# Gates of two streams packed into one half-width tile, and low parts at the GLU's start moved to GpSimd

## The chip, the cores and the metric

One core of a Trainium2 chip runs the whole kernel. The metric is the device time of one execution in microseconds (us), the median of several; less is better. The engines go by the profile's names: PE is TensorE's matmul and PEld its weight load, DVE is VectorE, ACT is ScalarE, POOL is GpSimd, SP is SyncE, whose queue (SPq) issues the DMAs.

## The reference

Two layers run over two streams, a latent of 256 tokens and a context of 256 tokens, both 1024 wide. Layer 0 mixes with a bidirectional S5 state-space scan followed by a GLU, layer 1 with a bidirectional gated DeltaNet over chunks of 64 tokens with 16 value heads. Each layer ends with a squared-ReLU MLP (the context's only in layer 0). The pieces that the change touches:

```python
# S5 layer, for each stream
y = gelu(y_forward + y_backward + d_skip * u)
y_a, y_b = split(y @ w_glu, 2);  out = y_a * sigmoid(y_b)
# gated DeltaNet layer, for each stream: 4 x 16 gate columns of w_in
gl = rest[..., qk + vd:].reshape(b, l, 2, 2, 16)      # (beta | g) x (forward | backward) x head
beta = sigmoid(gl[:, :, 0])
g = -exp(a_log) * softplus(gl[:, :, 1] + dt_bias)
g_b = cumsum(blocks(g), axis=-1)                      # within chunks of 64 tokens
```

## The kernel before

Matmuls run in a 32-bit format of reduced precision, so every operand is split in a high part and a low part (the rest), and every product is three matmuls (`mm3`: high by high, high by low, low by high). The high part is a cast on ScalarE, the low part a subtraction on VectorE or GpSimd.

**Order.** The kernel is written as tasks (generators). `drive` advances the task whose next step could start first by a clock of estimated durations (`Clock`), with priorities; each engine gets its instructions in the order that this and the tile framework's scheduler give, and works through them in that order. So an instruction that waits holds up all that is queued behind it on its engine. In the DeltaNet stage the clock also fills gaps in an engine's estimated time.

**Start of the GLU (some 205 to 330 us).** `y_split(s, b)` splits block b (of 8) of stream s of the S5 output, yT, into yh (ScalarE) and yl (VectorE) for all 16 (s, b); s = 0 is the context. `w_load` loads the 32 GLU weight blocks on SP's queue into four buffers (wraw), `w_split` makes whi on ScalarE and wlo in two halves of 128 x 512, the first on GpSimd, the second on VectorE (`loeng`). `glu(0, ...)` then takes weight blocks in order; one block meets two of the eight yT blocks, 12 matmuls of 512 columns. At the same time `s5_out(b, 1)` brings out the latent's eight blocks: TensorE, VectorE (sum, transposes, copies of states Hs) and ScalarE (GELU).

**Start of the DeltaNet stage (some 738 us on).** `w_load`, `w_split` and `gdn_proj` run through 48 projection blocks of 128 columns, the gates' own block third, after the first two query blocks. A projection of both streams takes 512 columns a matmul, of the latent alone 256; the gates' block does its two streams one after the other, in the order (1, 0), each with 24 matmuls of 256 columns into its half of one PSUM bank. The block has 4 groups of 32 rows, of which the upper 16 are zero columns of the weights: beta forward, beta backward, g forward, g backward, 16 heads each. Convolution and SiLU of each projection (`conv_silu`: four multiply-adds cacc and four or two products on VectorE, the rest on ScalarE) free the PSUM bank.

`gdn_gates` works on 128 x 512 tiles (tiles named gt; columns are the context's 256 tokens, then the latent's 256): log-sigmoid and softplus by exp, a reciprocal and a polynomial on VectorE; scans along the tokens, one for each direction; four DMAs write the summed decays GR to DRAM (grd); four transposes (gtp) and 32 small matmuls (glp, decays at the chunks' ends) go through PSUM, and VectorE copies them out. From the gates' block on, GpSimd makes all low parts of the weights in four quarters (`alone`). Behind the gates, `gdn_t(p, d)` computes for each head pair p and direction d a triangular inverse: it reads X from grd by DMA, GpSimd adds a mask, VectorE subtracts (X, gpn), and with the keys' products (kks, from transposes of the keys that share PSUM banks with gtp and glp) N, U and T follow in turns between VectorE, TensorE and ScalarE. `gdn_chain` runs the recurrences over the chunks, `gdn_read` and `gdn_out` the readout; the second MLP ends the kernel.

Of the kernel before, what the change touches and what calls it, by code (L numbers as in the profile page):

```python
# [978 lines left out]
def host_weights(i):  # L979
    a = {n: np.asarray(v) for n, v in i.items()}  # L980
    out = {}
    w = a["s5_w_glu"][0].reshape(8, 128, 2, 4, 256)
    out["w_glu"] = w.transpose(3, 0, 1, 2, 4).reshape(4, 4, 2, 128, 512).transpose(0, 1, 3, 2, 4).reshape(4, 4, 128, 1024)
    out["w1"] = a["mlp_w1"].reshape(2, 4, 2, 128, 8, 512).transpose(0, 4, 1, 3, 2, 5).reshape(2, 8, 4, 128, 1024)
    out["w2"] = a["mlp_w2"].reshape(2, 8, 4, 128, 1024)
    wi = a["gdn_w_in"][0]
    out["w_in"] = wi[:, :6144].reshape(8, 128, 48, 128).transpose(2, 1, 0, 3).reshape(48, 128, 1024)
    wg = np.zeros((1024, 4, 32), np.float32)
    wg[:, :, :16] = wi[:, 6144:].reshape(1024, 4, 16)
    out["w_gate"] = wg.reshape(8, 128, 128).transpose(1, 0, 2).reshape(128, 1024)  # L990
    gb = np.zeros((2, 4, 32), np.float32)
    gb[0, 2:, :16] = a["gdn_dt_bias"][0]
    gb[1, 2:, :16] = a["gdn_a_log"][0]
# [25 lines left out]
class K2(K):  # L1019
# [100 lines left out]
    def w_split(self, blocks):  # L1120

        nc = self.nc
        for _, shape, *dst in blocks:
            if not dst:
                yield from self.hslot.take()
            while not self.raws:
                yield HOLD
            raw, _, t = self.raws.pop(0)
            yield t
            hi, lo = dst or [self.wr.tile([128, 1024], F32R, name=n, tag=n, bufs=self.nhi) for n in ("whi", "wlo")]  # L1130
            nc.scalar.copy(hi, raw)

            n = 4 if self.loeng[0] is self.loeng[1] is nc.gpsimd else 2
            for j in range(n):
                h = slice(j * 1024 // n, (j + 1) * 1024 // n)
                self.loeng[2 * j // n].tensor_tensor(lo[:, h], raw[:, h], hi[:, h].bitcast(F32), op=OP.subtract)
            self.wslot.give()
            (self.wout if dst else self.wq).append([t.rearrange("p (a b) -> p a b", a=shape[0]) for t in (hi, lo)])
            yield
# [8 lines left out]
    def y_split(self, s, b):  # L1148
# [6 lines left out]
        nc.vector.tensor_tensor(nat(self.yl), src, nat(self.yh).bitcast(F32), op=OP.subtract)  # L1155
# [126 lines left out]
def s5_phase(ctx, k):  # L1282

    nc = k.nc
    with ExitStack() as cs:
# [119 lines left out]
        ld, sp = T(k.w_load(blocks), 0, [], "sync"), T(k.w_split(blocks), 0, [], "scalar")  # L1405
# [22 lines left out]
def host_consts2():  # L1428
# [17 lines left out]
    c[:, M_G] = np.where(r % 32 >= 16, 0.0, np.where(r < 64, -1.0, 1.0))  # L1446
    c[:, M_G + 1] = (r % 32 < 16) & (r >= 64)
# [9 lines left out]
class K3(K2):  # L1457
# [48 lines left out]
    def gdn_gates(self, tmp, o):  # L1506
# [7 lines left out]
        def t():  # L1514
            tag = next(room)
            return (self.gb.tile([128, 512], F32, name="gt", tag=tag) if tag == "N" else
                    self.gw.tile([128, 512], F32, name="gt", tag=tag, bufs=NRB))
# [4 lines left out]
        V.tensor_scalar(s, ps, gs, gc[:, 0:1], op0=OP.mult, op1=OP.add)  # L1522
# [30 lines left out]
        for d in range(2):  # L1553
            r = slice(64 + 32 * d, 96 + 32 * d)
            G.memset(m[r], 1.0)
            G.memset(m[r, (0 if d == 0 else 63):512:64], 0.0)
            f = lambda x: x[r] if d == 0 else bass.AP(tensor=x.tensor, offset=x[r].offset + 511, ap=[list(x[r].ap[0]), [-1, 512]])
# [12 lines left out]
        for k in range(8):  # L1570
            for d in range(2):
                c = k if d == 0 else (3 - k if k < 4 else 11 - k)
                last = c * 64 + (63 if d == 0 else 0)
                o = k * 32 + d * 16
                nc.tensor.matmul(lp[:, o:o + 16], GR[64:128, last:last + 1].to_broadcast([64, 128]),
                                 self.ident[64:128, 64 + 32 * d:64 + 32 * d + 16], start=(k == 0 and d == 0), stop=(k == 7 and d == 1),
                                 skip_group_check=True)
        gt = t().rearrange("p (a b c d) -> p a b c d", a=4, b=2, c=2)
        V.tensor_copy(gt.rearrange("p a b c d -> p (a b c d)"), tp)
# [4 lines left out]
        V.tensor_tensor(self.gp, gt[:, :, 1, :, 0:16], gt[:, :, 0, :, 0:16], op=OP.subtract)  # L1584
# [4 lines left out]
        V.tensor_copy(gn, gt[:, :, 1, :, 0:16])  # L1589
# [19 lines left out]
    def gdn_proj(self, streams, out):  # L1609

        while not self.wq:
# [6 lines left out]
        for n, s in enumerate(streams):  # L1618
            o = ps if s is None else ps[:, 256 * s:256 * s + 256] if len(streams) > 1 else ps[:, 0:256]
            for dt in range(8):  # L1620
                self.mm3(o, wh[:, dt], wl[:, dt], self.cols(self.hh, dt, s), self.cols(self.hl, dt, s), dt == 0, dt == 7)
# [424 lines left out]
    def gdn_phase(self, tmp, gb, hp, new):  # L2046
# [42 lines left out]
        def gate():  # L2089
            j = proj(I["w_gate"], (1, 0), 0, o)  # L2090
# [174 lines left out]
```

## Time and profile before

| | us |
|---|---|
| median of 3 runs | 1602.71 |
| lowest, highest | 1600.59, 1606.34 |
| profiled execution | 1608.33 |
| its span | 1606.5 |
| PE busy (share of span) | 1461.4 (91%) |
| DVE busy | 1098.4 (68%) |
| ACT busy | 775.2 (48%) |
| POOL busy | 652.0 (41%) |

The rows below were taken from the profiled execution; times in them count from its span's start. In a timeline a row is a run of like instructions: start, time until the last ends, engine, line, operation, output and inputs with shapes, count, and in brackets the idle time before it and who ended it. All instructions carry line L273, that of the helper that issues them, so groups go by the names of tiles. A waits view says who waited for whom. PE's busy time contains overlaps of pipelined matmuls.

### The profile page before, as it was taken

The page shows a single profiled execution, that of the slowest core. Times are in us where ns is not written, and L with a number is a line of the kernel's source. Part 1 is how long each engine was busy: PE and PEld are TensorE (multiplying, and loading weights), DVE is VectorE, ACT ScalarE, POOL GpSimd, SP SyncE. Part 2 cuts the span into 40 slices and gives each one's busy share as a digit, 9 for nine tenths or more (in the row PEclk, how much of TensorE's full clock was granted, in tenths as well). Part 3 has the DMA queues.
Part 4 walks back from the last instruction along what each step waited for, and adds up shares of the span by engine and source line. Part 5 has one row for each costly group of instructions (what it writes and reads, how often), then busy time and mean ns, then how long its engine had stood idle before and what let it go on. Part 6 is the DMA issues. An engine that isn't in the chain of part 4 may idle for free. (4 is left out here: it accounts for less than half of the span.)

```text
span 1606.5 us, 31329 instructions
## 1 busy us (share of the span) xinstructions
PE 1461.4 (91%) x12370; PEld 1115.2 (69%) x12370; DVE 1098.4 (68%) x2036; ACT 775.2 (48%) x1635; POOL 652.0 (41%) x590
## 2 busy tenths in 40 slices
PE   6895689989999999996978998989998999989998
PEld 2474457768777777786756775767776665789997
DVE  6999877754334333448998876686978775666766
ACT  3262675534222223315456655656665755564443
POOL 4962026623333332335777543443543400024432
PEclk8897789989999999998889999989998999999999
DMA  8758725454444454422222211111121112535552
GB/s 286 255 195 200 141 86 184 151 183 134 163 162 166 163 187 161 152 91 66 90 70 67 67 54 48 50 51 54 61 70 38 45 58 79 188 127 194 185 186 92
DMA packets 76771, 200.77 MB, mean 125 GB/s; under 512 B 8784, under 2 KB 29008, under 8 KB 76368
## 3 DMA queue, kind: packets, MB, share of 16 engines
q1 hardware_dynamic: 76112, 197.78, 38.3%
q8 instruction: 97, 1.59, 0.4%
q10 hardware_dynamic: 512, 0.98, 0.2%
q14 instruction: 50, 0.41, 0.1%
HBM read 192.71 MB, written 6.03 MB: 124 GB/s over the span
## 5 line engine op out<-in xcount | busy, mean ns | idle before, releaser
L273 ACT CAST whi<-wraw 128x1024 fp32r<-128x1024 f32 x221 | 225.6, 1045 | 255.7 <-PE w L273 139.0
L273 POOL TENSOR_TENSOR wlo<-wraw,whi 128x256 fp32r<-128x256 f32 (+1 forms) x221 | 206.8, 963 | 270.7 <-ACT whi L273 253.2
L273 DVE TENSOR_TENSOR wlo<-wraw,whi 128x1024 fp32r<-128x1024 f32 (+1 forms) x189 | 223.4, 1210 | 81.5 <-ACT whi L273 80.6
L273 PE MATMUL w<-hh,whi 128*128 128x256 f32 (+1 forms) x512 | 170.4, 335 | 0.0
L273 PE MATMUL w<-hl,whi 128*128 128x256 f32 (+1 forms) x512 | 169.3, 332 | 0.0
L273 PE MATMUL w<-hh,wlo 128*128 128x256 f32 (+1 forms) x512 | 168.9, 332 | 0.0
L273 POOL TENSOR_TENSOR sq<-rl 128x512 f32<-128x512 f32 (+1 forms) x64 | 62.7, 980 | 216.1 <-ACT rl L273 212.1
L273 PE MATMUL w<-whi,h1h 128*128 128x512 f32 x384 | 148.9, 395 | 0.0
L273 PE MATMUL w<-whi,h1l 128*128 128x512 f32 x384 | 148.5, 390 | 0.0
L273 PE MATMUL w<-wlo,h1h 128*128 128x512 f32 x384 | 148.4, 389 | 0.0
L273 PE MATMUL proj<-hh,whi 128*128 128x256 f32 (+1 forms) x360 | 132.4, 368 | 7.4 <-ACT pp L273 6.7
L273 DVE TENSOR_TENSOR ma<-w,g 128x512 f32<-128x512 f32 x96 | 65.3, 687 | 103.0 <-PE w L273 102.9
L273 PE MATMUL proj<-hh,wlo 128*128 128x256 f32 (+1 forms) x360 | 127.8, 355 | 1.2 <-POOL wlo L273 1.2
L273 PE MATMUL proj<-hl,whi 128*128 128x256 f32 (+1 forms) x360 | 127.3, 354 | 0.0
L273 POOL TENSOR_TENSOR xr<-xr,ma 128x512 f32<-128x512 f32 x56 | 82.2, 1471 | 95.1 <-DVE ma L273 95.1
L273 DVE SCALAR_TENSOR_TENSOR cacc<-pp,cw,cacc 128x520 f32<-128x520 f32 (+1 forms) x128 | 112.3, 879 | 9.6 <-ACT cacc L273 8.0
L273 ACT ACTIVATE v<-c,vsc 64x128 f32<-64x128 f32 x224 | 80.7, 362 | 62.8 <-PE c L273 57.7
L273 PEld LDWEIGHTS w<-hh,whi 128*128 128x128 f32 x512 | 98.0, 192 | 18.3 <-DVE wlo L273 4.2
L273 DVE TENSOR_TENSOR h1l<-sq,h1h 128x512 fp32r<-128x512 f32 (+1 forms) x64 | 36.3, 568 | 104.5 <-POOL sq L273 102.1
L273 PEld LDWEIGHTS w<-hl,whi 128*128 128x128 f32 x512 | 98.5, 192 | 10.5 <-issue 1.9
L273 PEld LDWEIGHTS w<-hh,wlo 128*128 128x128 f32 x512 | 98.3, 192 | 9.8 <-issue 0.8
L273 POOL TENSOR_TENSOR rstd<-ms,mhalf 128x1 f32<-128x1 f32 (+2 forms) x22 | 17.3, 788 | 179.1 <-DVE ms L273 163.4
(316 smaller groups left out, 3492.2 us busy)
## 6 DMA issues: line engine op xcount, KB each, us to landing
wraw<-in_w_dram SPq DMA_DIRECT2D x128, 512.0 KB, 4.5
adaw<-in_ada_w_dram SPq DMA_DIRECT2D x92, 512.0 KB, 4.8
wraw<-in_w_in_dram SPq DMA_DIRECT2D x48, 512.0 KB, 3.2
wraw<-in_w_glu_dram SPq DMA_DIRECT2D x32, 512.0 KB, 3.4
wraw<-in_w_out_dram SPq DMA_DIRECT2D x16, 512.0 KB, 3.4
Kt<-kd SPq DMA_DIRECT2D x32, 128.0 KB, 6.5
X<-grd SPq DMA_DIRECT2D x32, 128.0 KB, 3.2
V<-in_ada_w_dram SPq DMA_DIRECT2D x4, 512.0 KB, 5.2
```

The costliest lines, as they stand in the source:

```text
L273: r = f(*args, **kw)
```

## The change

**Gates.** The weights' zero columns change places with the used ones: in each group of 32 the used 16 are now the upper 16. For the latent (s = 1) the matmul takes the block's 128 columns as they are; for the context (s = 0) it takes a window that begins 16 columns later, so the context's gates land in rows 0 to 15 of each group and the latent's in rows 16 to 31, each meeting zeros of the other. Both streams accumulate into one 128 x 256 region; the last window is 112 columns wide. The order of the streams is (0, 1). All tiles of `gdn_gates` are 256 columns wide; the scans cover 256 tokens of both streams at once; the DMAs into grd are eight (one for each direction, parity and stream) with half the data; the transposes are two; two operations on the transposed gates (gp, gn) are done for each stream.

**GLU.** `y_split` makes the context's low parts on GpSimd, the latent's on VectorE as before. `w_split(blocks, 3)` makes both halves of the first three GLU weight blocks' low parts on GpSimd.

```diff
-    wg[:, :, :16] = wi[:, 6144:].reshape(1024, 4, 16)
+    wg[:, :, 16:] = wi[:, 6144:].reshape(1024, 4, 16)
...
-                self.loeng[2 * j // n].tensor_tensor(lo[:, h], raw[:, h], hi[:, h].bitcast(F32), op=OP.subtract)
+                (nc.gpsimd if nb < first else self.loeng[2 * j // n]).tensor_tensor(lo[:, h], raw[:, h], hi[:, h].bitcast(F32), op=OP.subtract)
...
-        nc.vector.tensor_tensor(nat(self.yl), src, nat(self.yh).bitcast(F32), op=OP.subtract)
+        (nc.vector if s else nc.gpsimd).tensor_tensor(nat(self.yl), src, nat(self.yh).bitcast(F32), op=OP.subtract)
...
-        ld, sp = T(k.w_load(blocks), 0, [], "sync"), T(k.w_split(blocks), 0, [], "scalar")
+        ld, sp = T(k.w_load(blocks), 0, [], "sync"), T(k.w_split(blocks, 3), 0, [], "scalar")
...
-                    self.gw.tile([128, 512], F32, name="gt", tag=tag, bufs=NRB))
+                    self.gw.tile([128, 512], F32, name="gt", tag=tag, bufs=NRB))[:, 0:256]
...
-        V.tensor_scalar(s, ps, gs, gc[:, 0:1], op0=OP.mult, op1=OP.add)
+        V.tensor_scalar(s, ps[:, 0:256], gs, gc[:, 0:1], op0=OP.mult, op1=OP.add)
...
-            G.memset(m[r, (0 if d == 0 else 63):512:64], 0.0)
+            G.memset(m[r, (0 if d == 0 else 63):256:64], 0.0)
...
-                r = 64 + 32 * d + h2
-                dst = bass.AP(tensor=self.grd.tensor, offset=self.grd.offset + 8192 * d + 64 * h2, ap=[[1024, 8], [128, 8], [1, 64]])
-                nc.sync.dma_start(dst, GR[r:r + 16:2].rearrange("p (c i) -> p c i", i=64))
+                for s in range(2):
+                    r = 64 + 32 * d + 16 * s + h2
+                    dst = bass.AP(tensor=self.grd.tensor, offset=self.grd.offset + 8192 * d + 64 * h2 + 512 * s, ap=[[1024, 8], [128, 4], [1, 64]])
+                    nc.sync.dma_start(dst, GR[r:r + 15:2].rearrange("p (c i) -> p c i", i=64))
...
-        for b in range(4):
+        for b in range(2):
             nc.tensor.transpose(tp[:, b * 128:b * 128 + 128], GR[:, b * 128:b * 128 + 128], self.ident)
...
-        V.tensor_tensor(self.gp, gt[:, :, 1, :, 0:16], gt[:, :, 0, :, 0:16], op=OP.subtract)
+        for s in range(2):
+            V.tensor_tensor(self.gp[:, 2 * s:2 * s + 2], gt[:, :, 1, :, s], gt[:, :, 0, :, s], op=OP.subtract)
...
-        V.tensor_copy(gn, gt[:, :, 1, :, 0:16])
+        for s in range(2):
+            V.tensor_copy(gn[:, 2 * s:2 * s + 2], gt[:, :, 1, :, s])
...
-            o = ps if s is None else ps[:, 256 * s:256 * s + 256] if len(streams) > 1 else ps[:, 0:256]
+            o = ps if s is None else ps[:, 0:256]
...
+                    wide = 128 if s or dt < 7 else 112
+                    lh, ll = [w.rearrange("p a b -> p (a b)")[:, 128 * dt + 16 - 16 * s:128 * dt + 16 - 16 * s + wide] for w in (wh, wl)]
+                    for m, (l, x) in enumerate(((lh, self.hh), (lh, self.hl), (ll, self.hh))):
+                        nc.tensor.matmul(o[0:wide], l, self.cols(x, dt, s), start=n == dt == m == 0, stop=n == 1 and dt == 7 and m == 2,
+                                         skip_group_check=True)
...
-            j = proj(I["w_gate"], (1, 0), 0, o)
+            j = proj(I["w_gate"], (0, 1), 0, o)
```

## Rows read from the trace of the kernel before

**Rows 1.** the page's busy times: busy us, share of the span, instructions

```profile
PE 1461.4 (91%) x12370; PEld 1115.2 (69%) x12370; DVE 1098.4 (68%) x2036; ACT 775.2 (48%) x1635; POOL 652.0 (41%) x590
```

**Rows 2.** busy time by stretch: us, then PE, PEld, DVE, ACT, POOL busy

```profile
753.00:786.00 33.00, 29.39 (x154) 24.54 (x152) 31.22 (x40) 16.36 (x37) 29.02 (x37) 0.95 0.24 82
786.00:805.00 19.00, 18.83 (x90) 15.86 (x90) 18.72 (x35) 10.21 (x26) 9.08 (x9) 0.82 0.26 85
805.00:825.00 20.00, 12.89 (x75) 9.95 (x74) 17.77 (x21) 10.41 (x22) 17.81 (x16) 0.90 0.25 79
825.00:850.00 25.00, 20.91 (x223) 17.62 (x222) 23.14 (x39) 14.75 (x34) 15.79 (x18) 0.81 0.15 47
```

**Rows 3.** waits of PE from 805 to 850: us, times, longest

```profile
PE ap L273 <- DVE T L273: 6.3, 2, 3.6
PE proj L273 <- ACT pp L273: 3.5, 1, 3.5
```

**Rows 4.** waits of PE from 204 to 262

```profile
PE glu L273 <- ACT whi L273: 1.9, 2, 1.2
PE glu L273 <- POOL wlo L273: 1.5, 2, 1.1
PE yp L273 <- ACT Hs L273: 0.7, 1, 0.7
```

**Rows 5.** busy time of the gate tiles alone, 753 to 806

```profile
753.00:806.00 53.00, 5.52 (x36) 5.20 (x36) 24.33 (x27) 1.05 (x2) 1.26 (x4) 0.90 0.25 82
```

**Rows 6.** groups of VectorE's instructions, shapes apart, 753 to 806

```profile
L273 DVE SCALAR_TENSOR_TENSOR gt<-gt 128x512 f32<-128x512 f32 x9 | 9.4, 1044 | 0.2
L273 DVE RECIPROCAL gt<-gt 128x512 f32<-128x512 f32 x1 | 3.4, 3353 | 0.0
L273 DVE TENSOR_TENSOR_SCAN gt<-gt 32x512 f32<-32x512 f32 x2 | 3.2, 1610 | 0.1
L273 DVE SCALAR_TENSOR_TENSOR zs<-zth,proj 128x256 f32<-128x256 f32 x1 | 0.4, 406 | 0.0
```

**Rows 7.** timeline of VectorE: start, us, instruction

```profile
796.14 0.68 DVE L273 TENSOR_TENSOR X<-X,gpn 128x512 f32<-128x512 f32 x1
803.27 0.42 DVE L273 COPY gt<-glp 128x256 f32<-128x256 f32 x1
813.18 1.82 DVE L273 TENSOR_TENSOR N<-X,kks 128x512 f32<-128x512 f32 x2
```

**Rows 8.** timelines of VectorE, TensorE, SP's queue and GpSimd

```profile
743.29 1.37 DVE L273 TENSOR_TENSOR hl<-hf,hh 128x512 fp32r<-128x512 f32 x1 [1.55 <-ACT hh L273]
...
746.25 0.28 PE L273 MATMUL proj<-hh,whi 128*128 128x256 f32 x1
...
783.64 2.99 SPq L273 DMA_DIRECT2D grd<-gt  x4
...
790.82 2.90 POOL L273 TENSOR_TENSOR X<-X,c 128x512 f32<-128x512 f32 x2 [4.33 <-DMA X<-grd]
```

**Rows 9.** instructions on tile yl: duration ns min/median/max

```profile
L273 DVE TENSOR_TENSOR yl<-yT,yh x16: 619/642/1736, 209.8 to 249.7; 128x256 fp32r<-128x256 f32 x16
```

**Rows 10.** timelines of TensorE, VectorE and GpSimd at the GLU's start

```profile
213.99 0.50 PE L273 MATMUL glu<-whi,yh 128*128 128x512 f32 x1
217.52 0.39 PE L273 MATMUL glu<-whi,yh 128*128 128x512 f32 x1
...
209.81 3.35 DVE L273 TENSOR_TENSOR yl<-yT,yh 128x256 fp32r<-128x256 f32 x4
213.08 1.89 DVE L273 TENSOR_TENSOR wlo<-wraw,whi 128x512 fp32r<-128x512 f32 x3
...
207.32 3.73 POOL L273 TENSOR_TENSOR wlo<-wraw,whi 128x512 fp32r<-128x512 f32 x3 [76.69 <-ACT whi L273]
240.40 0.75 POOL L273 TENSOR_TENSOR gm<-gm,g 128x256 f32<-128x256 f32 x1 [4.84 <-DVE gm L273]
```

**Rows 11.** busy time of a later stretch, columns as in rows 2

```profile
960.00:1000.00 40.00, 32.44 (x417) 23.74 (x416) 27.73 (x66) 20.03 (x51) 14.38 (x16) 0.91 0.19 61
```

More of the change, by code (lines that the diff above doesn't have):

```diff
@@ L988, in host_weights @@
     wg = np.zeros((1024, 4, 32), np.float32)
-    wg[:, :, :16] = wi[:, 6144:].reshape(1024, 4, 16)
+    wg[:, :, 16:] = wi[:, 6144:].reshape(1024, 4, 16)
     out["w_gate"] = wg.reshape(8, 128, 128).transpose(1, 0, 2).reshape(128, 1024)
     gb = np.zeros((2, 4, 32), np.float32)
-    gb[0, 2:, :16] = a["gdn_dt_bias"][0]
-    gb[1, 2:, :16] = a["gdn_a_log"][0]
+    for r in (slice(0, 16), slice(16, 32)):
+        gb[0, 2:, r] = a["gdn_dt_bias"][0]
+        gb[1, 2:, r] = a["gdn_a_log"][0]
     out["gcol"] = gb.reshape(2, 128).T
@@ L1118, in w_load, with w_split @@
             yield self.clock.t["sync"]
-    def w_split(self, blocks):
+    def w_split(self, blocks, first=0):
         nc = self.nc
-        for _, shape, *dst in blocks:
+        for nb, (_, shape, *dst) in enumerate(blocks):
             if not dst:
@@ L1445, in host_consts2 @@
     r = np.arange(128)
-    c[:, M_G] = np.where(r % 32 >= 16, 0.0, np.where(r < 64, -1.0, 1.0))
-    c[:, M_G + 1] = (r % 32 < 16) & (r >= 64)
+    c[:, M_G] = np.where(r < 64, -1.0, 1.0)
+    c[:, M_G + 1] = r >= 64
     return c
@@ L1555, in gdn_gates @@
             G.memset(m[r], 1.0)
-            G.memset(m[r, (0 if d == 0 else 63):512:64], 0.0)
-            f = lambda x: x[r] if d == 0 else bass.AP(tensor=x.tensor, offset=x[r].offset + 511, ap=[list(x[r].ap[0]), [-1, 512]])
+            G.memset(m[r, (0 if d == 0 else 63):256:64], 0.0)
+            f = lambda x: x[r] if d == 0 else bass.AP(tensor=x.tensor, offset=x[r].offset + 255, ap=[list(x[r].ap[0]), [-1, 256]])
             V.tensor_tensor_scan(f(GR), f(m), f(lg), 0.0, op0=OP.mult, op1=OP.add)
@@ L1572, in gdn_gates @@
                 c = k if d == 0 else (3 - k if k < 4 else 11 - k)
-                last = c * 64 + (63 if d == 0 else 0)
+                last = c % 4 * 64 + (63 if d == 0 else 0)
                 o = k * 32 + d * 16
                 nc.tensor.matmul(lp[:, o:o + 16], GR[64:128, last:last + 1].to_broadcast([64, 128]),
-                                 self.ident[64:128, 64 + 32 * d:64 + 32 * d + 16], start=(k == 0 and d == 0), stop=(k == 7 and d == 1),
+                                 self.ident[64:128, 64 + 32 * d + 16 * (c // 4):64 + 32 * d + 16 * (c // 4) + 16], start=(k == 0 and d == 0), stop=(k == 7 and d == 1),
                                  skip_group_check=True)
-        gt = t().rearrange("p (a b c d) -> p a b c d", a=4, b=2, c=2)
-        V.tensor_copy(gt.rearrange("p a b c d -> p (a b c d)"), tp)
+        gt = t().rearrange("p (a b c s d) -> p a b c s d", a=2, b=2, c=2, s=2)
+        V.tensor_copy(gt.rearrange("p a b c s d -> p (a b c s d)"), tp[:, 0:256])
         gl = t()[:, 0:256].rearrange("p (a b c) -> p a b c", a=8, b=2)
@@ L1609, in gdn_proj @@
     def gdn_proj(self, streams, out):
+        nc = self.nc
         while not self.wq:
@@ L1618, in gdn_proj @@
         for n, s in enumerate(streams):
-            o = ps if s is None else ps[:, 256 * s:256 * s + 256] if len(streams) > 1 else ps[:, 0:256]
+            o = ps if s is None else ps[:, 0:256]
             for dt in range(8):
-                self.mm3(o, wh[:, dt], wl[:, dt], self.cols(self.hh, dt, s), self.cols(self.hl, dt, s), dt == 0, dt == 7)
+                if len(streams) == 1:
+                    self.mm3(o, wh[:, dt], wl[:, dt], self.cols(self.hh, dt, s), self.cols(self.hl, dt, s), dt == 0, dt == 7)
+                else:
+                    wide = 128 if s or dt < 7 else 112
[3 more added lines that the diff above has]
+                                         skip_group_check=True)
                 if dt == 7 and n == len(streams) - 1:
```

## The prediction

> **What bounds the kernel now.** I read the page's busy times first: TensorE is busy 91% of the span [rows 1], so over the whole kernel only its idle time and its slow-clock time can be had. The next view is the busy time by stretch, taken where the change sits. The gated-delta stage opens with the gates. From 753 to 805 us VectorE is busy 31.22 of 33 and 18.72 of 19 us, and TensorE 29.39 and 18.83: both are nearly full, GpSimd too in the first of them (29.02 of 33) [rows 2]. From 805 to 850 VectorE stays full (17.77 of 20 and 23.14 of 25) but TensorE has 7.1 and 4.1 us without work [rows 2]. So VectorE, which began late, is the engine that ends last there. The view of TensorE's waits for that stretch says the same: 6.3 us for the transposes T of the first triangular inverse (VectorE) and 3.5 us for the projection's bank, which ScalarE empties in order behind the convolution on VectorE [rows 3]. The reader should see that VectorE time taken out before 805 is worth something only after 805, and at most the 11.2 us that TensorE is idle there, plus the little before.
>
> The other half of the change sits at the start of the GLU, about 205 to 262 us. There TensorE's waits that this part can touch are small: 1.9 us for the high parts of the weights, 1.5 us for their low parts, 0.7 us for the state copies [rows 4]; 4.1 us together.
>
> **The gates.** The 128 x 512 tile (16 used rows of each 32) becomes a 128 x 256 tile with all rows used. VectorE spends 24.33 us in 27 instructions on these tiles [rows 5]. The largest: nine scalar_tensor_tensor 9.4, one reciprocal 3.4, two scans 3.2 [rows 6]. What one saves by half the columns: a 256-column operation of two inputs takes 0.41 us [rows 6], the 512-column subtraction from X takes 0.68 us [rows 7], so 0.28 us each where nothing holds it up. Nine times 0.28 is 2.5; the reciprocal is long enough to go by columns, half of 3.35 is 1.7; the scans half of 3.2, 1.6; the eight other wide ones (products, scalings, copies out of PSUM) at 0.2 on average, 1.6, an estimate from the same 0.28 with the cheaper one-input forms below it. Sum 7.4. Added are one more subtraction and one more copy on the packed transposes, at most 0.4 each for half-width operations (the 256-column price), so 0.4 to 0.8; I take 0.5. **VectorE saves 6.9 us.** The upper bound is half of the 24.33 less 0.5, 11.7 us: the nine run at 1.04 us on average against the 0.68 of an undisturbed one [rows 6, 7], so GpSimd holds them up, and fewer columns may shorten that as well. I take the lower end, since GpSimd's own list in that stretch (29.02 of 33 us [rows 2]) is hardly shorter afterwards.
>
> How much of 6.9 reaches the end. Between 786 and 805 TensorE is full (18.83 of 19), so the projections themselves don't come earlier; what comes earlier is what VectorE owes the first inverse: the copy of the last decays, now at 803.27, in a PSUM bank that the key transposes need next, and through them the mask product N at 813.18 [rows 7], from which T follows. I let 5.5 of 6.9 us through, about half of TensorE's 11.2 idle us; the bounds are 2 (TensorE is so full that the projections set the pace) and 11 (all its idle time goes).
>
> Smaller pieces of this part. The projection keeps its 48 matmuls of 256 columns each; the shifted weight windows change which rows receive, not the columns streamed. Zero. Its order of streams turns round, context first: the context's last low part starts at 743.29 and takes 1.37 us, and the block's first matmul is at 746.25 [rows 8], 1.6 us later; were the block pulled earlier by more than that, it would wait for the rest. Two transposes fewer on TensorE and shorter memsets on GpSimd: below 1 us, beside other work. **Eight writes of the decays instead of four** on SP's queue: four take 2.99 us [rows 8], so four more add 3.0 us; behind them on SP wait the four reads X and then the weight loads, which run four buffers ahead; GpSimd waits for X (4.33 us [rows 8]) with the next weight block's low part queued behind it. X's data is used at 796.14 [rows 7], and GpSimd's two additions on it, started at 790.82, take 2.90 [rows 8], so they end 2.4 us before: the 3.0 us would cost 0.6 if the scans ended when they do now. They end some 5 us or more earlier, so I cost it at nothing; without that cover it costs 0.6 us on VectorE's queue.
>
> **The GLU.** Eight low parts of the context move from VectorE (0.64 us median [rows 9]) to GpSimd, where a 256-column product takes 0.75 [rows 10]; three weight blocks' second halves (1.89 us for three on VectorE) go to GpSimd at 1.24 each, by its own 3.73 for three [rows 10]. VectorE loses 8 x 0.64 + 1.89 = 7.0 us, GpSimd gains 8 x 0.75 + 3.73 = 9.7 us. VectorE begins its first four low parts only at 209.81, behind the latest transposes, while GpSimd begins its halves at 207.32 [rows 10], so the first low parts can begin earlier on GpSimd, not later. The first GLU matmul is at 213.99 [rows 10]. After: if three low parts (2.3 us) are done by 207.3, where GpSimd starts on the weights now, then both halves of blocks one to three, 2.5 us each, at 210, 212.5 and 215, and the other five low parts between them, 3.8 us, so about 219 for the last. A block feeds 12 matmuls, and 15 of them go by from 213.99 to 217.52 [rows 10], 0.235 us each, so 2.8 us a block: from 214 the third is wanted at 219.6. It holds, with under a us to spare for the last low part. TensorE has the S5 outputs of the latent to do between the blocks in any order, so an earlier GLU only changes the order of its work. What can go are the 4.1 us of waits [rows 4]; VectorE's 7 free us bring the latent's transposes forward and with them ScalarE's casts. I take 1 us of gain; bounds 4.1 of gain and 3 of loss (GpSimd late by a block, 2.5 us, and a little more).
>
> What VectorE does while GpSimd works: the low part's times run from 0.62 to 1.74 us [rows 9], and the first of the four at 209.81 met GpSimd's third half, which ran to 211.05 [rows 10]. The Trainium skill (SBUF — State Buffer, section Who interferes with whom) says that a VectorE instruction with two SBUF inputs and a GpSimd instruction that reads SBUF exclude one another for the whole instruction. With that rule the trace agrees (1.74 against 0.62). By it the freed 7.0 us would be worth nothing wherever GpSimd's 9.7 fall on VectorE's work; the price is worked out in rival (e).
>
> **Sum.** 5.5 + 1 = 6.5 us. Against the profiled execution, 1608.33 us with a span of 1606.5, that is 1601.8. That execution is 5.6 us above the median of the runs shown, 1602.71; the same gain from the median gives 1596.2, which I predict as 1596.
>
> **Rivals.** (a) *The relief is absorbed.* TensorE is full from 786 to 805 [rows 2], and the planner may put convolution work into VectorE's free time whose projections come no earlier; then only some 2 us reach the end, or 1 with the GLU giving nothing: 1601, no change. For it: TensorE's 29.39 of 33; against: 11.2 idle us right behind. (b) *Slower: a new hole from the planner.* The order of the whole stage is written from estimated times, and these halve for some 20 instructions, so every later choice may fall otherwise. At the heads' boundaries TensorE already has holes, as 960 to 1000: 32.44 of 40, 7.6 us [rows 11]. One hole more of that size, with the gates' gain absorbed as in (a): +7.6 - 2 = +5.6, 1608. It decides from the point where TensorE's idle time behind 880 us grows by more than the VectorE time saved before. Against it: a hole may as well vanish. (c) *It doesn't do what it says:* the gate instructions hardly shrink, because their time is waiting for GpSimd rather than columns: 24.33 falls by the reciprocal and scans alone, 3.3 us, some 2.5 at the end, and the GLU 1: 1599, no change. (d) *More:* the upper bounds, or a hole that vanishes: 11 + 4.1, 1588. (e) *The move to GpSimd gives VectorE nothing:* each of the 11 added GpSimd instructions (eight low parts, three half blocks) can hold one VectorE operation up by 1.74 - 0.62 = 1.1 us [rows 9], up to 12 us against the 7.0 freed, so the GLU's 1 us is lost: 5.5, 1597, still faster. Against it: VectorE has nothing to do before 209.81 [rows 10].
>
> **How the numbers follow.** Chances: forecast 0.34 (own range 1592 to 1599), (a) 0.20, (b) 0.15, (c) 0.08, (d) 0.15, (e) 0.08. About 0.3%, 4.8 us, is what a measurement of this kernel can tell from no change. Faster by over that, below 1597.9: (d), nine tenths of the forecast and of (e), 0.53. Slower, above 1607.5: most of (b) and other losses of order, 0.15. Within: 0.32. The range must leave out no more than 2 in 10: from the upper bounds, 1586 (15.1 and a measurement's 1.6), to the hole's 1608.
>
> **What would show it.** Right: the gate tiles' VectorE time falls from 24.33 to about 17; the scans end before 780; TensorE's idle 11.2 us between 805 and 850 falls by half; the copy at 803.27 and N at 813.18 come 5 us earlier against the stage's start; the GLU begins at 214 or earlier, with GpSimd's three blocks done by 219. Wrong: the gate operations keep their means (c); N moves by less than 2 us (a); idle time of TensorE behind 880 us grows (b); TensorE waits for low parts of GpSimd's in the first GLU blocks by more than 2.5 us, which would turn the GLU part to a loss.

## The result: 24 us slower, and the profile after

The changed kernel takes 1627.72 us (median, 1623.58 to 1631.74), the kernel before beside it 1604.22; the ratio is 1.0147 with a 95% interval of 1.0124 to 1.0170. The profiled execution of the changed kernel took 1627.48 us, its span 1625.6. Forecast was 1596 with a range up to 1608: wrong in sign, and outside the range.

Since the stretch ahead of the gated-delta stage differs by several us from one execution to the next (in seven profiled kernels of this document that are alike up to there, the first projection starts at 731.8 to 740.0), times in the stage are given as distances from its first projection matmul, at 738.79 in before and 734.25 in after. From there to the end of the span it is 1606.5 - 738.79 = 867.7 us before and 1625.6 - 734.25 = 891.4 after: 23.6 us, the whole loss. This distance, the stage and all that follows it, is called the stage's time below.

The page's busy times, as [rows 1]:

```profile
PE 1474.8 (91%) x12368; PEld 1117.8 (69%) x12368; DVE 1088.8 (67%) x2027; ACT 775.6 (48%) x1635; POOL 665.2 (41%) x601
```

VectorE lost 9.6 us and GpSimd gained 13.2, in the direction meant; TensorE is busy 13.4 us longer with two instructions fewer. Busy time by stretch of after, the last two stretches of [rows 2] and that of [rows 11], shifted by 4.54 us so that they lie alike from the first projection:

```profile
800.46:820.46 20.00, 13.35 (x93) 9.92 (x91) 18.18 (x22) 11.61 (x28) 17.72 (x17) 0.96 0.33 105
820.46:845.46 25.00, 16.09 (x172) 13.59 (x172) 23.13 (x32) 10.48 (x19) 16.48 (x16) 0.76 0.21 64
955.46:995.46 40.00, 36.31 (x431) 27.28 (x431) 31.10 (x68) 20.31 (x52) 17.35 (x18) 0.91 0.18 60
```

TensorE was to be less idle in the first two of these stretches. It is more idle: 20 - 13.35 + 25 - 16.09 = 15.6 us against 11.2. TensorE's waits in these two (compare [rows 3]) show why:

```profile
PE up L273 <- DVE A L273: 10.8, 1, 10.8
PE ap L273 <- DVE T L273: 0.5, 1, 0.5
```

The wait for the first T is gone, and a longer one for A, two steps further in the same inverse, stands in its place. The gate tiles themselves, first their busy time by engine (as [rows 5]), then VectorE's groups (as [rows 6]):

```profile
743.00:800.00 57.00, 5.28 (x34) 5.07 (x34) 17.07 (x29) 0.84 (x2) 0.81 (x4) 0.91 0.26 85
```

```profile
L273 DVE SCALAR_TENSOR_TENSOR gt<-gt 128x256 f32<-128x256 f32 x9 | 6.0, 669 | 0.2
L273 DVE RECIPROCAL gt<-gt 128x256 f32<-128x256 f32 x1 | 1.7, 1748 | 0.0
L273 DVE TENSOR_TENSOR_SCAN gt<-gt 32x256 f32<-32x256 f32 x2 | 1.7, 868 | 1.5 <-POOL gt L273 1.5
```

24.33 us have become 17.07. VectorE's timeline, the copy of the last decays and N (as [rows 7]), and then what stands ahead of the first product A; behind it that A in the kernel before:

```profile
787.24 0.41 DVE L273 COPY gt<-glp 128x256 f32<-128x256 f32 x1
...
804.57 2.37 DVE L273 TENSOR_TENSOR N<-X,kks 128x512 f32<-128x512 f32 x2
...
817.73 2.87 DVE L273 SCALAR_TENSOR_TENSOR cacc<-pp,cw,cacc 128x520 f32<-128x520 f32 x1
820.51 1.64 DVE L273 TENSOR_TENSOR X<-X,gpn 128x512 f32<-128x512 f32 x1
822.08 4.36 DVE L273 SCALAR_TENSOR_TENSOR cacc<-pp,cw,cacc 128x520 f32<-128x520 f32 x3
826.35 1.28 DVE L273 TENSOR_TENSOR A<-ap,c 128x512 f16<-128x512 f32 x2
```

```profile
828.10 1.45 DVE L273 TENSOR_TENSOR A<-ap,c 128x512 f16<-128x512 f32 x2
```

The copy of the last decays (the first line) comes 11.5 us earlier than before (53.0 us behind the first projection instead of 64.5). N starts 70.3 us behind the first projection, 4.1 earlier than before. But ahead of A now stand a convolution step, the next pair's X and three more convolution steps, and A starts 92.1 us behind the first projection, where the kernel before has it 89.3 behind. The gain of N was spent before the inverse had made its second step. That this late A is what costs the 24 us doesn't follow: e4 below loses as much, and its first A starts 86.3 us behind the first projection, earlier than in before.

SP's queue and GpSimd (as [rows 8]): eight writes take 5.67 us instead of 2.99, and GpSimd's additions on X wait 0.31 and 0.30 us for their data instead of 4.33.

```profile
772.48 5.67 SPq L273 DMA_DIRECT2D grd<-gt  x8
...
783.65 1.39 POOL L273 TENSOR_TENSOR X<-X,c 128x512 f32<-128x512 f32 x1 [0.31 <-DMA X<-grd]
785.35 1.42 POOL L273 TENSOR_TENSOR X<-X,c 128x512 f32<-128x512 f32 x1 [0.30 <-DMA X<-grd]
```

The GLU's start. The tile yl (as [rows 9]) and GpSimd's timeline (as [rows 10]); TensorE's waits for low parts are the 1.5 us of [rows 4], as before:

```profile
L273 POOL TENSOR_TENSOR yl<-yT,yh x8: 863/916/1109, 202.3 to 216.2; 128x256 fp32r<-128x256 f32 x8
L273 DVE TENSOR_TENSOR yl<-yT,yh x8: 627/672/1739, 221.6 to 245.7; 128x256 fp32r<-128x256 f32 x8
```

```profile
202.27 2.51 POOL L273 TENSOR_TENSOR yl<-yT,yh 128x256 fp32r<-128x256 f32 x3 [74.08 <-ACT yh L273]
204.73 7.73 POOL L273 TENSOR_TENSOR wlo<-wraw,whi 128x512 fp32r<-128x512 f32 x6
212.41 4.74 POOL L273 TENSOR_TENSOR yl<-yT,yh 128x256 fp32r<-128x256 f32 x5
```

Last, where the 23.6 us come in. Busy time by stretch from the first projection on: 450 us, 150 us, and the rest, first of before, then of after (columns as in [rows 2]; the number in brackets behind each time is that of the instructions):

```profile
738.79:1188.79 450.00, 408.04 (x4256) 313.67 (x4256) 365.25 (x696) 268.47 (x674) 243.22 (x261) 0.94 0.19 61
1188.79:1338.79 150.00, 138.88 (x1873) 98.11 (x1868) 112.78 (x273) 93.75 (x260) 49.44 (x52) 0.97 0.15 49
1338.79:1606.50 267.71, 253.57 (x1541) 215.57 (x1539) 177.27 (x261) 130.56 (x229) 71.26 (x68) 0.98 0.48 158
```

```profile
734.25:1184.25 450.00, 398.68 (x4124) 304.78 (x4122) 351.81 (x667) 255.42 (x633) 235.91 (x254) 0.93 0.18 59
1184.25:1334.25 150.00, 136.15 (x1763) 94.67 (x1761) 115.99 (x266) 97.08 (x267) 54.38 (x57) 0.95 0.15 51
1334.25:1625.60 291.35, 274.08 (x1779) 226.76 (x1777) 190.39 (x301) 140.87 (x263) 72.29 (x69) 0.99 0.45 146
```

After 600 us TensorE has done 4256 + 1873 = 6129 matmuls before, and 4124 + 1763 = 5887 after: 242 fewer, and the rest takes 291.35 - 267.71 = 23.6 us longer. Over the three lines its idle time rises from 67.2 to 82.4 us, by 15.2; the other 8.4 are busy time. The granted clock is 0.93 and 0.95 in the first two stretches against 0.94 and 0.97, but 0.99 against 0.98 in the third, so what share of the 8.4 the clock has isn't shown. The idle time is in no single hole, and most of what was added lies early: 9.4 of the 15.2 us in the first 450 us, 2.7 and 3.1 in the other two stretches.

### The profile page after: what moved, and what is told of

Its sections match the earlier page's. It is cut to its first block, busy times and chain, and to the rows that moved or that the text cites. A ratio compares the mean times of both kernels' runs of the same rounds, so it can differ in the third digit from the quotient of the medians.

```text
span 1625.6 us, 31374 instructions
## 1 busy us (share of the span) xinstructions
PE 1474.8 (91%) x12368; PEld 1117.8 (69%) x12368; DVE 1088.8 (67%) x2027; ACT 775.6 (48%) x1635; POOL 665.2 (41%) x601
## 4 chain that ended last, share of the span: by engine, by line
PE 64%; DVE 17%; ACT 5%; POOL 5%; issue 4%; DMA 4%; SPq 1%; ACTq 0%; POOLq 0%; DVEq 0%
PE w L273 32%; PE proj L273 9%; PE c L273 7%; PE wo L273 3%; DVE cacc L273 3%; PE ada L273 2%; POOL wlo L273 2%; PE glu L273 2%; DVE U L273 2%; PE qs L273 1%; ACT whi L273 1%; PE up L273 1%; DVE X L273 1%; DVE W L273 1%; PE op L273 1%
## 5 line engine op out<-in xcount | busy, mean ns | idle before, releaser
L273 POOL TENSOR_TENSOR wlo<-wraw,whi 128x256 fp32r<-128x256 f32 (+1 forms) x224 | 211.2, 970 | 193.8 <-ACT whi L273 166.9
L273 DVE TENSOR_TENSOR wlo<-wraw,whi 128x1024 fp32r<-128x1024 f32 (+1 forms) x186 | 217.5, 1196 | 88.1 <-ACT whi L273 87.2
L273 DVE SCALAR_TENSOR_TENSOR cacc<-pp,cw,cacc 128x520 f32<-128x520 f32 (+1 forms) x128 | 118.2, 924 | 9.9 <-ACT cacc L273 8.3
L273 PEld LDWEIGHTS w<-hl,whi 128*128 128x128 f32 x512 | 97.7, 191 | 10.5 <-issue 1.9
```

What stands on the lines that cost most here:

```text
L273: r = f(*args, **kw)
```

## The experiments

Each gated-delta head pair needs a key block (projection, convolution, transposes, the key product kks), then the inverse (N, five rounds of T, A and U, and ub at its end), then the chains. The pairs are called first to eighth. Three theories went into the first four runs. A: the planner's order of the stage, written from estimated times, costs it. B: GpSimd's longer list at the GLU. C: the half-width gates themselves, with more instructions and DMAs.

**e1: the GLU half alone.** The kernel before with only these edits (lines shortened; w_split is called with 3, as in the change):

```diff
-                self.loeng[2 * j // n].tensor_tensor(lo ...
+                (nc.gpsimd if nb < first else self.loeng[2 * j // n]).tensor_tensor(lo ...
...
-        nc.vector.tensor_tensor(nat(self.yl) ...
+        (nc.vector if s else nc.gpsimd).tensor_tensor(nat(self.yl) ...
```

> The kernel before with the GLU half of the change alone (context's low parts and both halves of the first three weight blocks on GpSimd); gates as before, so the gated-delta stage is written in the order of before. Theory A (the loss is in the order of the gated-delta stage, which the planner writes from estimated times and which the gates' shorter estimates turn over): the first projection starts at 734, where it is in the changed kernel, in place of 738.7, and the time falls by the same 4 to 5 us, to about 1599. Theory B (GpSimd's longer list at the GLU does the harm, by holding VectorE up): no faster than before, 1604 or more.

Measured: 1603.69 us against 1605.16, ratio 0.9998 (0.9978 to 1.0018). No faster is what B expected by its words, and the gain that A expected isn't there; but B was to explain 24 us, and the GLU half alone loses nothing, so B falls as the cause. The stage takes 867.1 us, as in before.

**e2: the gates alone.** The changed kernel with those edits taken back.

> The changed kernel with the GLU half undone: half-width gates and their order of the gated-delta stage, low parts at the GLU as before. Theory A: slower than the changed kernel by the GLU's 4 to 5 us, about 1632. Theory B: about 1604 or, with the gates' saving, 1598. If neither half alone is slow, the two act together and both theories fall.

Measured: 1623.06 us, ratio 1.0120 (1.0092 to 1.0147); the stage 888.5 us. The loss is in the gates' half. It isn't 4 to 5 us larger than in the changed kernel, as A expected: the GLU's half gains nothing that can be told here either.

**e3: the new gates in the old order.** The changed kernel; the planner's clock books the gate instructions with the column count of before, four DMA writes and four transposes, and so writes its steps in exactly the order of before (the last line is shortened):

```diff
-        if not aps:
+        if not aps or self.free:
             return 0, 0
...
+        n *= self.mul; start = max( ...
```

(mul is 2 around the halved instructions, and free leaves out those that are new.) The framework's scheduler still sees the instructions as they are: TensorE's list is that of before for 150 matmuls of the stage's 7660 and then differs in places, and the seventh pair's key product stands behind 4336 matmuls, in before behind 4280.

> The changed kernel, all of it, but the planner books the gates' instructions at the width that they had before (double columns, four writes, four transposes, one subtraction and one copy), so the tasks of the gated-delta stage are emitted exactly in the order of before. Theory A: the loss is gone; GLU 4 to 5 us and up to 5.5 us of the gates gained, 1594 to 1600. Theory C (the half-width gates themselves cost: eight writes on SP's queue, another phase of the engines): still about 1628.

Measured: 1603.45 us, ratio 0.9984 (0.9965 to 1.0003), the stage 864.1 us. The loss is gone, and C with it; the 1594 to 1600 of A are missed, since the gains that it counted on don't come.

**e4: the old gates in the new order.** The converse: the kernel before, whose planner books half the columns, eight writes, two transposes and the context first. On the chip the gates are 512 wide.

> The kernel before, its instructions unchanged (gates 512 wide; only the gates' block takes its streams context first), but the planner books the gates at half the width, eight writes and two transposes, so the tasks are emitted in the order of the changed kernel. Theory A: slow by the order alone, about 1604 + 24, 1622 to 1634. Theory C: as before, about 1604.

Measured: 1629.46 us, ratio 1.0153 (1.0132 to 1.0175), the stage 894.2 us, inside what A expected.

The four together settle A against B and C: with the work of either kernel, the planner's old order of steps gives 864 to 868 us and its new one 888 to 894. In either the stage is 3 to 6 us shorter with the new gates (867.1 or 867.7 to 864.1; 894.2 to 891.4 or 888.5), by one profile each; the medians don't tell the first pair apart (1603.45 against 1603.69).

**e5 to e8: other orders of the same work.** What in the order costs the time? In VectorE's timeline the key products and the inverses of the seventh and eighth pair moved most. Of before (kks of the seventh and eighth pair, N of the eighth, and the ends ub of the inverses of the sixth, the seventh and the eighth):

```profile
1195.56 0.42 DVE L273 TENSOR_TENSOR kks<-kk,c 128x256 f32<-128x256 f32 x1
...
1234.70 0.68 DVE L273 SCALAR_TENSOR_TENSOR ub<-wp,U 128x512 f32<-128x512 f32 x1
...
1266.61 0.42 DVE L273 TENSOR_TENSOR kks<-kk,c 128x256 f32<-128x256 f32 x1
1267.06 1.84 DVE L273 TENSOR_TENSOR N<-X,kks 128x512 f32<-128x512 f32 x2
...
1279.89 0.65 DVE L273 SCALAR_TENSOR_TENSOR ub<-wp,U 128x512 f32<-128x512 f32 x1
...
1321.16 0.69 DVE L273 SCALAR_TENSOR_TENSOR ub<-wp,U 128x512 f32<-128x512 f32 x1
```

and of after:

```profile
1231.61 0.68 DVE L273 SCALAR_TENSOR_TENSOR ub<-wp,U 128x512 f32<-128x512 f32 x1
...
1233.23 0.42 DVE L273 TENSOR_TENSOR kks<-kk,c 128x256 f32<-128x256 f32 x1
...
1295.79 0.41 DVE L273 TENSOR_TENSOR kks<-kk,c 128x256 f32<-128x256 f32 x1
...
1296.93 1.81 DVE L273 TENSOR_TENSOR N<-X,kks 128x512 f32<-128x512 f32 x2
1298.66 0.68 DVE L273 SCALAR_TENSOR_TENSOR ub<-wp,U 128x512 f32<-128x512 f32 x1
...
1343.03 0.68 DVE L273 SCALAR_TENSOR_TENSOR ub<-wp,U 128x512 f32<-128x512 f32 x1
```

Before, the seventh pair's kks is there at 1195.56, while the sixth inverse still runs to 1234.70, so the two inverses overlap; N of the eighth starts at 1267.06 while the seventh's ub ends at 1279.89. After, the seventh's kks comes at 1233.23, when the sixth inverse has just ended (1231.61), and the eighth's at 1295.79, three us ahead of the seventh's last ub: the last inverses run one behind the other. In distances from the first projection the eighth's kks goes from 527.8 to 561.5 us. Theory D: this late end of the last inverse sets the end of the kernel. Rival E: orders from the halved estimates are bad in any case. The constant from which the planner starts its clock in the stage shuffles the order and leaves every instruction as it is (what is expected counts places in TensorE's list in matmuls of the chains):

```diff
-GDN0 = 803.4465179647354
+GDN0 = 806.4465179647354
```

(e5; minus 2 in e6; on the kernel before, minus 0.5 in e7 and plus 0.5 in e8.)

> The changed kernel; only the constant from which the planner starts its clock in the gated-delta stage is 3 us later. Every instruction is the same, only the order that the planner writes moves: the product of keys of the seventh and of the eighth head pair (kk) stands behind 447 and 563 matmuls of the chains in TensorE's list, against 443 and 568 in the kernel before and 498 and 621 in the changed one. Theory D (the late place of the last two key blocks sets the end of the stage): from the first projection to the end 864 to 870 us, so some 1603 in all, the 24 us are gone without touching the estimates. Rival E (orders written from the halved estimates are late whatever the start): 1620 to 1630.

Measured: 1612.07 us, ratio 1.0055 (1.0027 to 1.0084), the stage 871.0 us. The stage is 20 us shorter than with after's order, one us beyond what D said; the median in all was 9 above it, and so 15.7 below that of the changed kernel.

> The changed kernel with the planner's start constant 2 us earlier. The same two products stand behind 530 and 670 chain matmuls. From two orders with the same gates, the eighth at 568 with 864 us and at 621 with 890 us from the first projection to the end, a chain matmul is worth about 0.5 us. Theory D: 890 + 49 x 0.5 = 914, so 1640 to 1655 in all. Rival E: no different from the changed kernel, 1620 to 1630.

Measured: 1659.41 us, ratio 1.0351 (1.0312 to 1.0390), the stage 919.1 us: D's sign, 5 us above its price for the stage and 4 above its range in all.

> The kernel before with the planner's start constant 0.5 us earlier; instructions and estimates are those of before. The two products stand behind 518 and 630 chain matmuls (443 and 568 in the kernel before). Theory D: 867 + 62 x 0.5 = 898 us from the first projection to the end, so 1630 to 1640 in all: the kernel before then owes its time to a lucky order, and not to its estimates. Rival E (the old estimates give good orders): within 5 us of before.

Measured: 1617.54 us, ratio 1.0105 (1.0067 to 1.0143), the stage 877.0 us: slower, but by a third of what D's price gave (9 us more than before, not 31).

> The kernel before with the planner's start constant 0.5 us later; the two products stand behind 449 and 588 chain matmuls. Theory D: 867 + 20 x 0.5 = 877, so about 1612 to 1616 in all. Rival E: within 5 us of before. If it is the seventh product's place alone that counts (449 against 443), also within 5 us of before.

Measured: 1618.20 us, ratio 1.0113 (1.0078 to 1.0148), the stage 883.9 us, 7 more than D's price gave.

E falls: an order from the halved estimates can be 20 us better or 28 us worse in the stage than that of the changed kernel, and half a us on the untouched kernel's constant costs 15 us to either side (1617.54 and 1618.20 against 1602.42 for the kernel before beside them). The place in TensorE's list is a poor price, though. e7 has its last key product behind 630 chain matmuls and e8 behind 588, and e8 is the slower in the stage; their kks come 544.6 and 545.0 us behind the first projection, at the same time. In all profiles so far the span's end followed the end of the last inverse; whether that end is a cause or only a mark was put to the test by moving it.

**e9: the eighth pair's key product delayed.** The kernel before with one line longer (the addition; 26 times for p == 7, none for the other pairs):

```diff
+; [self.nc.nc.gpsimd.tensor_scalar(kks, kks, 1.0, None, op0=OP.mult) for _ in range(26 if p == 7 else 0)]
```

> The kernel before, with 26 in-place multiplications by one on GpSimd (128 x 256 each, some 0.8 us) on the eighth head pair's key product kks, between VectorE's writing it and the mask product N that opens the last triangular inverse; the planner doesn't see them, TensorE's order up to that key product is that of before. Theory D (the end of the last inverse sets the end of the stage, 282 to 291 us ahead of the span's end in all eight profiles so far): N of the last pair some 20 us later, the last ub at about 600 us after the first projection instead of 582, the span 15 to 20 us longer, 1618 to 1624 in all. Rival F (a late last key block only marks an order that loses time in many places; the block itself has slack): within 5 us of before.

Measured: 1627.22 us, ratio 1.0140 (1.0119 to 1.0162), the stage 891.0 us. The instructions on the tile kks (count: min/median/max ns, first and last start), then VectorE's timeline (kks, N, last ub of the eighth pair):

```profile
L1720 POOL TENSOR_SCALAR kks<-kks x26: 845/851/859, 1261.1 to 1300.8; 128x256 f32<-128x256 f32 x26
```

```profile
1260.59 0.42 DVE L273 TENSOR_TENSOR kks<-kk,c 128x256 f32<-128x256 f32 x1
...
1305.03 1.29 DVE L273 TENSOR_TENSOR N<-X,kks 128x512 f32<-128x512 f32 x2
...
1340.37 0.69 DVE L273 SCALAR_TENSOR_TENSOR ub<-wp,U 128x512 f32<-128x512 f32 x1 [0.53 <-PE wp L273]
```

Between kks and N now lie 44 us, more than the 26 x 0.851 = 22, because weight low parts and others on GpSimd stand between them. The last ub is at 607.2 us from the first projection instead of 582.4, 24.8 later, and the span ends 23.3 later (7 and 3 us more than expected). Up to this kks every engine's list is that of before; behind it the framework's scheduler, which sees the 26 instructions, writes another one. No wait of TensorE from 1260 to 1360 names GpSimd, so the loss isn't GpSimd's longer list by itself. One late key product can cost as much as the changed kernel lost. It isn't the same loss, though: busy time from 550 to 625 us behind the first projection, of before and then of e9 (columns as in [rows 2]):

```profile
1288.79:1363.79 75.00, 71.65 (x754) 46.12 (x753) 47.70 (x133) 42.58 (x120) 4.81 (x6) 1.00 0.20 66
```

```profile
1283.17:1358.17 75.00, 64.28 (x666) 39.75 (x663) 41.67 (x100) 31.15 (x85) 21.53 (x22) 0.77 0.10 33
```

TensorE is idle 10.7 us instead of 3.4 here, and its granted clock falls from 1.00 to 0.77. Over the stage 8.6 of the 23.3 us are idle time and 14.7 busy time of the same matmuls, while the changed kernel lost 15.2 and 8.4, most of the first ahead of the last two pairs.

**e10: the fifth pair's instead**, the same line with p == 4.

> The same 26 multiplications on the fifth head pair's kks instead, three pairs ahead of the end. Theory D: TensorE has other projections, chains and inverses to do meanwhile, and the time moves only by what the last inverse's end moves, 0 to 10 us: 1603 to 1614, less than the delay on the eighth pair, and the span still ends 282 to 291 us behind the last ub. If any lost time anywhere in the stage counts in full: 1620 or more, as with the eighth.

Measured: 1607.85 us, ratio 1.0013 (0.9995 to 1.0032), the stage 866.7 us. VectorE's kks and N of the fifth pair, and the last ub:

```profile
1052.29 0.42 DVE L273 TENSOR_TENSOR kks<-kk,c 128x256 f32<-128x256 f32 x1
...
1101.24 1.29 DVE L273 TENSOR_TENSOR N<-X,kks 128x512 f32<-128x512 f32 x2
...
1315.17 0.69 DVE L273 SCALAR_TENSOR_TENSOR ub<-wp,U 128x512 f32<-128x512 f32 x1
```

N starts 49 us behind kks (2.3 in before), and the last ub is at 581.2 us, the end where it was. Three pairs ahead of the end the same delay, and more of it, costs nothing that can be told. The framework's scheduler took part in that: behind the delay the lists differ from those of before, and the last key product stands behind 5041 matmuls instead of 5165.

**e11: the last two key blocks taken out of the way** in the changed kernel (parts of lines):

```diff
-st["kks"]
+(self.stt[p - 1] if p > 5 else st)["kks"]
...
-            kk = T(self.prep_kk(p, st[p])
+            kp = kk if p else None; kk = T(self.prep_kk(p, st[p])
...
-[g, zero, kk]
+[g, zero, kk if p < 6 else kp]
```

(the same for kqs).

> The changed kernel, in which the inverses of the seventh and the eighth head pair take the key products (kks and kqs) of the pair before them, so that neither waits for its own late key block; that part of the computation is another one, its amount is the same. The planner's order is the same up to the sixth pair. In TensorE's list the last inverse's end then stands behind some 702 us of work, against 710 in the changed kernel and 704 to 706 in those orders that were fast. Theory D: the last ub at 585 to 592 us after the first projection instead of 605 to 609, so 870 to 880 us from there to the end and 1606 to 1614 in all. Rival F: as the changed kernel, 1620 to 1630.

Measured: 1618.18 us, ratio 1.0078 (1.0049 to 1.0107), the stage 880.9 us, 10.5 less than the changed kernel. N of the eighth pair, its own kks, which it no longer waits for, and the last ub:

```profile
1245.01 1.29 DVE L273 TENSOR_TENSOR N<-X,kks 128x512 f32<-128x512 f32 x2
...
1297.78 0.42 DVE L273 TENSOR_TENSOR kks<-kk,c 128x256 f32<-128x256 f32 x1
...
1323.30 0.69 DVE L273 SCALAR_TENSOR_TENSOR ub<-wp,U 128x512 f32<-128x512 f32 x1 [0.53 <-PE wp L273]
```

N starts 53 us ahead of that kks, and the last ub is at 588.0 us instead of 608.8. In the middle of what was expected for ub, a us above it for the stage, and 4 above it for the median, which so lies between D's range and F's. Nearly half of the loss comes back; the sixth pair and those ahead of it are as late as in the changed kernel. So is TensorE: in the first 450 us, of which e11 touches only the last 16, it is idle 50.4 us, against 51.3 in the changed kernel and 42.0 in before:

```profile
735.29:1185.29 450.00, 399.62 (x4114) 305.06 (x4112) 351.67 (x668) 255.90 (x631) 239.37 (x256) 0.92 0.18 59
```

**e12: another start, picked by D** in the changed kernel (the constant minus 3.25).

> The changed kernel with the planner's start constant 3.25 us earlier: of some 50 starts of the changed kernel that were looked at, one of the three whose last key product stands early in TensorE's list, behind 645 us of work (649 in the kernel before, 667 in the changed one; the seventh pair's 588 against 580 and 612). Theory D: 866 to 878 us from the first projection to the end, 1602 to 1612 in all. Rival E (orders from the halved estimates are late): 1620 or more.

Measured: 1604.95 us, ratio 1.0002 (0.9982 to 1.0023), the stage 870.6 us. The changed kernel, in an order whose last key product comes early, is level with the kernel before (the stage 2.9 us longer).

All fourteen profiles, each time from its own first projection (us):

| kernel | last ub starts | end of span | difference |
|---|---|---|---|
| e3, new gates, old order | 576.1 | 864.1 | 288.0 |
| e5 | 580.3 | 871.0 | 290.7 |
| e1, GLU alone | 580.7 | 867.1 | 286.4 |
| e10 | 581.2 | 866.7 | 285.5 |
| e12 | 581.4 | 870.6 | 289.2 |
| before | 582.4 | 867.7 | 285.3 |
| e11 | 588.0 | 880.9 | 292.9 |
| e7 | 590.5 | 877.0 | 286.5 |
| e8 | 596.7 | 883.9 | 287.1 |
| e2, gates alone | 606.1 | 888.5 | 282.4 |
| e9 | 607.2 | 891.0 | 283.8 |
| after | 608.8 | 891.4 | 282.6 |
| e4, old gates, new order | 609.6 | 894.2 | 284.5 |
| e6 | 629.2 | 919.1 | 289.9 |

The last inverse ends over a span of 53 us; the end follows it at 282 to 293 us. e9 and e10 show that a delay put on the last pair's key product moves both, and that one on the fifth pair's moves neither. The table alone doesn't show that the last chain is the cause in every row: what TensorE loses ahead of it moves both columns as well. In the changed kernel e11 puts some 10.5 of the 23.6 us on the key blocks of the last two pairs; the other 13 it leaves. No version beats both kernels by more than can be told: e3 is the nearest, 0.16% below before with an interval that reaches no change.

## Why the prediction was wrong

**The reading of the gates was right.** VectorE's time on them fell by 7.3 us; 6.9 were forecast. That the two are so near is partly luck: without one copy that took 2.23 us here (last section; 0.41 at the full width in before), it would have been 9.2. The nine scalar_tensor_tensor gave 0.38 us each (0.28 forecast), the reciprocal 1.6 (1.7), the scans 1.5 (1.6). Rival (c), instructions that hardly shrink, is out. The scans start at 771.77 and were to end before 780. The eight writes added 2.7 us (3.0), and the cover named for them held: GpSimd waits less for X than before.

**What reaches the end was forecast at 5.5, between 2 and 11.** N came 4.1 us earlier, about the 5 that were named. In the planner's old order the stage is 3.0 to 3.6 us shorter (e3 against e1 and before, one profile each), inside the bounds and below the value taken; the medians don't tell it from none. This term alone would have been a small miss, and no change by the measure of 0.3%.

**The step that failed is the price and the chance of rival (b), "a new hole from the planner".** It was put at one hole of 7.6 us, +5.6 in the sum, chance 0.15, with the remark that a hole may as well vanish; the forecast's own sum, 6.5 us of gain, held no term for the order. Rival (b) was right in kind, and its sign of decision was met: behind 880 us (141.2 from the first projection) TensorE's idle time grew from 47.1 to 56.3 us, by 9.2 against 7.3 saved on VectorE. Two things were wrong in it. First, the price was taken from one hole at a head boundary [rows 11], and that hole got smaller (36.31 us busy of 40 instead of 32.44). The planner's new order cost 26.5 us of the stage with the work as it was (e4), 23.6 in the changed kernel and 51 in e6. Of the 23.6, some 10.5 hang on the last two key blocks and inverses (e11), a chain that I didn't follow back from the end of the last inverse; e9 shows that a delay there reaches the end. The other 13 stay with e11, and no run took them apart; what the profiles show of them is that TensorE was idle 9.4 us more in the stage's first 450 us, ahead of the last two pairs. Second, a loss was taken to be as likely as a gain. Half a us on the planner's constant makes the untouched kernel 1.05% and 1.13% slower (e7, e8): its order was better than those two beside it, and none of the other orders tried beat it by more than can be told. What (b) took over from (a), that the gates' gain is absorbed, was seen at the stage's head: VectorE's free time was filled with convolution steps ahead of A.

**The GLU was forecast at 1 us of gain, between 4.1 and a loss of 3.** Measured alone it is -0.02% (-0.22 to +0.18), 3.5 us of gain to 2.9 of loss, so the sign stays open and the bounds hold. By the steps: the first three low parts took 2.51 us (2.3 forecast) and ended ahead of 207.3; the three blocks 7.73 (7.5), to 212.5; the other five low parts 4.74 (3.8), to 217.2, ahead of the 219 that were said to be in time. On GpSimd a low part takes 0.916 us, not the 0.75 of the row used. TensorE's waits for low parts stayed at 1.5 us. Rival (e) can't be told from the forecast at this size, but VectorE's own low parts still run from 0.627 to 1.739 us, as before the change.

**Rival (d)** named "a hole that vanishes"; no order here showed a gain of its size.

**What stays open.** Why the planner places the last key blocks late from the one set of estimates and early from another was not followed through its choices. That before's order is better than its neighbours is shown for two of them, which were chosen, not drawn: what share of all orders is slower isn't known. Nor was it tried which of the pairs ahead of the last two holds the half that e11 left; that most of TensorE's added idle time lies there is read from the profiles and was not tested.

## What to carry to other kernels

Where a program writes the order of a long stage from estimated times, price an edit of any estimate as a new draw of that order: measure the spread first, by shuffling the unchanged kernel with a constant that changes no instruction (here -0.5 and +0.5 us cost 15 us each), and measure the edit itself with the old order held fixed. Then look for the last serial chain of the stage, here the last key product and inverse: a delay of 49 us three pairs earlier cost nothing that could be told, one of 44 us on the last cost 23. Look at the idle time ahead of it too: in the changed kernel 9.4 of the 15.2 us added lay there. And see whether time saved at the head of a stage is filled by work of a later use ahead of the chain that it was to shorten: in the changed kernel it was, and the first A came 2.8 us later than before; in e3 it wasn't, and A came 4.5 us earlier.

## What the hardware showed that was not expected

A copy of 64 x 256 within SBUF took VectorE 2.23 us in the changed kernel; in e2, e3, e5, e6, e11 and e12 the same copy took 0.28 to 0.29 us. In the long case GpSimd ran six memsets back to back over it (GpSimd's timeline, then VectorE's):

```profile
764.09 1.58 POOL L273 MEMSET v<- 128x256 f32 x6
...
763.59 2.23 DVE L273 COPY gt<-gt 64x256 f32<-64x256 f32 x1
```

The copy began at 763.59, while GpSimd was in a subtraction that ended at 764.16, and ended 0.15 us behind the last memset (765.67). The Trainium skill (SBUF — State Buffer, section Who interferes with whom) says that copies can enter a mode in which VectorE and GpSimd exclude one another for a whole instruction, and that the one issued later waits. With that the row agrees in kind, and so do e1 and e10, where the copy of the old width (64 x 512) began inside a GpSimd subtraction, ended some 0.3 us behind it and took 0.95 and 0.96 us instead of 0.41. But the copy of 2.23 us, if its own work took its usual 0.28, stood behind the subtraction and at least five memsets in a row, not behind one instruction. It is a single sighting that no run here took apart.
